# Last experts in steps of 1024 inner columns with 4 KB gate and up rows, 64 slots for the fifth place, one more ring place

## The chip, the core and the metric

The program runs on one core of a Trainium2 chip. The metric is the device time of one execution in microseconds (us). Before the change, three runs gave 2216.11, 2219.05 and 2222.17 us; their median is 2219.05 us. A change of under 0.3% (6.7 us) can't be told from none.

## What is computed

The reference passes 256 tokens of width 1024 (one x of 256 x 1024 in f32) through two blocks: a recurrent mixer and a first mixture of experts, then attention, a dense feed-forward layer, a state-space layer and a second mixture of experts. The change touches only this last layer:

```python
xt = _rms_norm(x, norm_g).reshape(-1, d)
logits = xt @ w_router                       # 256 tokens, 8 experts
top_vals, top_idx = lax.top_k(logits, 2)
gates = softmax(top_vals)
...
def expert_block(args):
    xb, e = args
    return (silu(xb @ w_gate[e]) * (xb @ w_up[e])) @ w_down[e]
...
out = segment_sum(ys * slot_w, slot_tok)
return x + out
```

w_gate and w_up are 1024 x 3584 per expert, w_down is 3584 x 1024, all f32: 44.04 MB for an expert, 352.3 MB for the eight. Each token goes to two of the eight experts, so the experts have 512 tokens in all.

## The kernel before

The last layer is the class `Moe2`. Tokens of one expert are gathered into slots (`gather`, a product with a 0/1 matrix), in blocks of 32: an expert has 2, 3 or 4 blocks, that is 64, 96 or 128 slots. The program is fixed ahead of the data, so the number of blocks belongs to a place in a ranking: expert 0 has place 0, the other seven have places 1 to 7 by falling number of tokens. `BLOCKS` gives the blocks by place, `PLACES` the order in which the places are worked through. In that order the experts have 3, 2, 4, 2, 3, 3, 2 and 3 blocks; they are called the first to the eighth here. Tokens that find no slot are counted (`n_over`), and if there are any, `general` computes them after the loop, with all experts' weights read again for each half of the tokens.

`experts` is the loop, 7 steps per expert, each over 512 of the 3584 inner columns. A step does these things in TensorE's order: half of the gate and up products (`project`, contraction over 512 of the 1024 features, two loads of 1 MB), the four transposes of the step before (`hidden_T`), the other half of gate and up, and then the down products of the step before (`down`, two loads). In between, ScalarE and VectorE make the hidden values of the step (`hidden`: silu of gate times up). A product has 32 slots as its stationary operand and 512 columns of weights as the moving one, and four of them run side by side in four column groups of the array. So the products of a step grow with the blocks: 144 matmul instructions for three blocks, 96 for two. For three blocks the third block's products take column groups of a second PSUM bank (L2710), and `third` copies half of that bank to SBUF, so that the two halves of its sums can be added.

All weights come through a ring of SBUF places of 8 KB per partition (1 MB in all), filled by SyncE's DMA queue in the order of the list that `loads` makes. A gate or up load takes 512 rows and 512 columns, so its contiguous runs in DRAM are 2 KB; a down load takes for each partition two adjacent rows of 1024 columns, 8 KB. A place is filled again as soon as its products are through (`done` calls `ahead`, which issues the next load); the ring has 15 places in this layer: 2 that are there from the start, 3 of the pool opened before the feed-forward layer, 4 of this layer's own (`K.slots(sp, 4, 3)` in `body`), and 6 that held split weights earlier.

PSUM has 8 banks: two hold an expert's output sums through all of its steps (one for two blocks), the gate and up sums take two (one) per 512 columns, and transposes, gathers and the combining products take one each. `combine` multiplies an expert's output by the gate weights and adds it to x, for the expert before during the second step of the next. After the last expert x is stored.

Of the kernel before, what the change touches and what calls it, by code (L numbers as in the profile page):

```python
# [2423 lines left out]
class Moe2(Phase):  # L2424
# [5 lines left out]
    BLOCKS = (3, 4, 3, 3, 3, 2, 2, 2)  # L2430
# [6 lines left out]
    def loads(cls, K):  # L2437
# [7 lines left out]
        def load(nm, e, k0, c0):  # L2445
            def fn(t):
                K.nc.sync.dma_start(t, expert(nm, e)[:, k0 * 128:(k0 + 4) * 128, c0:c0 + 512].rearrange("e (c p) f -> p (e c) f", p=128))  # L2447
                return 512
            return fn, False

        def rows(e, f, h):

            def fn(t):
                w = expert("down", e)[:, f * 512:(f + 1) * 512].rearrange("e (p q) c -> p (e q) c", q=4)
                K.nc.sync.dma_start(t.rearrange("p q c -> p (q c)").rearrange("p (q c) -> p q c", q=2), w[:, 2 * h:2 * h + 2])  # L2455
                return 512
            return fn, False

        steps = [(e, f) for e in range(cls.E) for f in range(7)]
        for s in range(len(steps) + 1):  # L2460
            if s < len(steps):
                e, f = steps[s]
                out += [load(nm, e, k0, f * 512) for k0 in (0, 4) for nm in ("gate", "up")]
            if s:
                out += [rows(*steps[s - 1], h) for h in range(2)]
# [9 lines left out]
    def route(self):  # L2475
# [9 lines left out]
        xT = K.rows_T(K.x, K.vec["moe_norm_2"], lambda: self.t("xT", [P, 8, P], 2))  # L2485
# [100 lines left out]
    def general(self):  # L2586
# [9 lines left out]
        with tc.If(self.n_over > 0):  # L2596
            for b in range(2):
                xw, hT = self.t("g_xn", [128, D], 2, tag="xg"), self.t("g_hT", [128, 8, 128], 2, tag="xT")
# [16 lines left out]
    def experts(self):  # L2615
        K = self.K
        n = 7 * self.E
# [4 lines left out]
        for s in range(n + 1):  # L2622
            e, f = s // 7, s % 7
            if s == 4:
                K.order += [K.nc.values_load(self.number[0:1, i:i + 1], engines=[mybir.EngineType.SP], min_val=0, max_val=self.E - 1) for i in range(1, self.E)]
            if s == 20:
                self.n_over = K.count(self.n_int)
            if f == 3 and e + 1 < self.E:
# [3 lines left out]
            if s < n:  # L2632
                gu = self.project(e)
                next(gu)
                next(nxt, None)
            if s:
                hid = self.hidden_T(hs.pop(s - 1), (s - 1) // 7)
            if s < n:
                hs[s] = self.hidden(drive(gu), e)
                next(nxt, None)  # L2640
            if s:
                self.down((s - 1) // 7, (s - 1) % 7, hid)
# [69 lines left out]
    def project(self, e):  # L2712
# [18 lines left out]
    def hidden(self, ps, e):  # L2731
        nc, nb = self.K.nc, self.blocks(e)
        h = self.t("h", [128, 512], 2)
        if nb == 4:
            nc.scalar.activation(h, ps[0], AF.Silu)
            nc.vector.tensor_tensor(h, h, ps[1], OP.mult)
            return h
        if nb == 3:
            t, g, u = self.third(ps[1]), self.t("third_g", [32, 512]), self.t("third_u", [32, 512])
            nc.vector.tensor_tensor(g, t[0:32], ps[1][0:32], OP.add)  # L2740
            nc.vector.tensor_tensor(u, t[32:64], ps[1][32:64], OP.add)
        nc.scalar.activation(h[0:64], ps[0][0:64], AF.Silu)  # L2742
        nc.vector.tensor_tensor(h[0:64], h[0:64], ps[0][64:128], OP.mult)  # L2743
        if nb == 3:
            nc.scalar.activation(g, g, AF.Silu)
            nc.vector.tensor_tensor(h[64:96], g, u, OP.mult)
        return h[0:32 * nb]

    def hidden_T(self, h, e):

        K, nc = self.K, self.K.nc
        S = 32 * self.blocks(e)
        p, hq = K.ps()[:, 0:4 * S], h.rearrange("s (p q) -> s q p", q=4)
        for j in range(4):
            nc.tensor.transpose(p[:, j * S:(j + 1) * S], hq[:, j], K.ident[0:S, 0:S])  # L2755
        hid = self.t("hid", [128, 4, 128], 2)[:, :, 0:S]
# [123 lines left out]
```

## Time and profile before

| | |
|---|---|
| runs | 2216.11, 2219.05, 2222.17 us |
| profiled execution, its own time | 2217.24 us |
| its span, first to last instruction | 2215.5 us |
| TensorE busy | 1965.2 us, 89% |
| VectorE, ScalarE, GpSimd busy | 730.1, 501.5, 165.1 us |
| DMA | 644.45 MB, mean 291 GB/s |
| granted clock, mean | 0.948 |

The profiled execution lies between the lowest run and the median, 1.8 us under the median. TensorE's busy time includes waits in the middle of a group, since ends of matmuls are modelled; the distance from one step's transposes to the next step's tells more than the busy share. The clock is a share of 2.4 GHz; 0.5 is the lower level, 1.2 GHz. The DMA share can read a little over 1, since packets of one engine overlap.

### The profile page before, as it was taken

Reading aid. Unit: us, or ns where it says so; the run is one execution under the profiler, and the core shown is the slowest. Engines: PE = TensorE matmul, PEld = TensorE weight load, DVE = VectorE, ACT = ScalarE, POOL = GpSimd, SP = SyncE. Lnnn points to the kernel's source line nnn. Section 1 sums busy time; section 2 is a strip of 40 time slices with the busy share of each in tenths; the row PEclk is TensorE's granted clock in tenths of the full one; section 3 lists DMA queues with packets and bytes.
Section 4 is the critical chain, followed back from the end, with each engine's and each line's share of the span. In section 5 each row is a group of like instructions: output and inputs, shape, how many; then the busy total and the mean of one; then the engine's idle time right before and its main releaser. Section 6 shows DMA issues by size and latency. Waiting matters only on the chain.

```text
span 2215.5 us, 35511 instructions
## 1 busy us (share of the span) xinstructions
PE 1965.2 (89%) x15104; PEld 1041.2 (47%) x15104; DVE 730.1 (33%) x1524; ACT 501.5 (23%) x917; POOL 165.1 (7%) x222
## 2 busy tenths in 40 slices
PE   7886888877777768889998689999999999999998
PEld 7765753323222356689997553333333333333232
DVE  6678841211201146554445732110001022211022
ACT  5452220100100035444444132110001111111111
POOL 3144100000000021000002410000000000000000
PEclk9998999989988989999999889999999999999999
DMA  6340459999999942165554099999989999999995
GB/s 201 116 136 20 154 190 362 421 419 390 419 418 420 408 141 96 58 219 186 179 188 153 1 337 358 387 397 397 392 286 398 397 396 398 396 398 397 398 394 222
DMA packets 220180, 644.45 MB, mean 291 GB/s; under 512 B 20606, under 2 KB 24108, under 8 KB 182124
## 3 DMA queue, kind: packets, MB, share of 16 engines
q1 hardware_dynamic: 219388, 641.13, 76.4%
q8 instruction: 122, 2.00, 0.4%
q0 software_dynamic: 336, 0.82, 0.1%
q14 instruction: 46, 0.38, 0.0%
q10 hardware_dynamic: 288, 0.13, 0.0%
HBM read 639.94 MB, written 1.05 MB: 289 GB/s over the span
## 4 chain that ended last, share of the span: by engine, by line
PE 51%; DVE 2%; DMA 1%; SPq 1%; POOL 0%; ACT 0%; issue 0%; POOLq 0%; ACTq 0%; DVEq 0%
PE ps L2705 28%; PE ps L2710 6%; PE ps L151 4%; PE ps L149 4%; PE ps L150 4%; PE ps L2755 1%; DMA w<-in_moe_w_up_dram 1%; PE ps L2789 1%; PE ps L2668 1%; DVE f L2356 1%; SPq L2447 1%; PE ps L2674 0%; DVE xs L2363 0%; SPq L2455 0%; PE ps L312 0%
## 5 line engine op out<-in xcount | busy, mean ns | idle before, releaser
L2705 PE MATMUL ps<-w,xg 128*32 128x512 f32 x4032 | 470.6, 594 | 4.7 <-DMA w<-in_moe_w_up_dram 3.7
L2705 PEld LDWEIGHTS ps<-w,xg 128*32 128x32 f32 x4032 | 124.4, 110 | 280.3 <-issue 260.5
L2705 PE MATMUL ps<-w,hid 128*32 128x512 f32 x2016 | 232.9, 593 | 0.6 <-ACT hid L2757 0.6
L120 DVE TENSOR_TENSOR wl<-w,wh 128x1024 fp32r<-128x1024 f32 (+1 forms) x146 | 174.2, 1237 | 179.7 <-ACT wh L119 179.7
L1547 PE MATMUL ps<-w,xg 128*32 128x512 f32 x1024 | 163.8, 674 | 51.3 <-DMA w<-in_moe_w_up_dram 42.0
L149 PE MATMUL ps<-hT,wh 128*128 128x256 f32 x704 | 204.8, 291 | 2.9 <-ACT wh L119 1.9
L151 PE MATMUL ps<-hT,wl 128*128 128x256 f32 x704 | 203.4, 289 | 0.5 <-DVE wl L120 0.5
L150 PE MATMUL ps<-hT,wh 128*128 128x256 f32 x704 | 203.2, 289 | 0.0
L119 ACT ACTIVATE wh<-w 128x1024 fp32r<-128x1024 f32 (+1 forms) x148 | 146.8, 1044 | 199.7 <-PE ps L150 110.1
L149 PEld LDWEIGHTS ps<-hT,wh 128*128 128x128 f32 x704 | 139.4, 198 | 4.5 <-ACT wh L119 2.3
L150 PEld LDWEIGHTS ps<-hT,wh 128*128 128x128 f32 x704 | 139.3, 198 | 0.3
L151 PEld LDWEIGHTS ps<-hT,wl 128*128 128x128 f32 x704 | 138.8, 197 | 0.8 <-DVE wl L120 0.8
L2740 DVE TENSOR_TENSOR third_g<-third,ps 32x512 f32<-32x512 f32 x28 | 18.9, 676 | 356.2 <-ACT third L2728 356.2
L2705 PEld LDWEIGHTS ps<-w,hid 128*32 128x32 f32 x2016 | 64.3, 110 | 145.5 <-issue 139.1
L1547 PE MATMUL ps<-w,hidT 128*32 128x512 f32 x512 | 96.0, 724 | 41.0 <-DMA w<-in_moe_w_down_dram 35.1
L2710 PE MATMUL ps<-w,xg 128*32 128x512 f32 x896 | 119.9, 592 | 0.0
L1547 PEld LDWEIGHTS ps<-w,xg 128*32 128x32 f32 x1024 | 36.8, 121 | 161.1 <-issue 73.8
L2743 DVE TENSOR_TENSOR h<-h,ps 64x512 f32<-64x512 f32 x49 | 33.8, 690 | 224.0 <-ACT h L2742 223.2
L2757 ACT ACTIVATE hid<-ps 128x384 f32<-128x384 f32 (+2 forms) x56 | 26.0, 463 | 354.5 <-PE ps L2755 354.2
L1547 PEld LDWEIGHTS ps<-w,hidT 128*32 128x32 f32 x512 | 20.8, 126 | 105.2 <-DMA w<-in_moe_w_down_dram 58.6
L1514 PEld LDWEIGHTS ps<-oh,xn 128*128 128x128 f32 x256 | 62.2, 334 | 16.2 <-issue 13.7
L1514 PE MATMUL ps<-oh,xn 128*128 128x128 f32 x256 | 65.3, 412 | 4.4 <-PEq L1457 3.5
(667 smaller groups left out, 2358.6 us busy)
## 6 DMA issues: line engine op xcount, KB each, us to landing
w<-in_moe_w_gate_dram SPq DMA_DIRECT2D x176, 1024.0 KB
w<-in_moe_w_up_dram SPq DMA_DIRECT2D x176, 1024.0 KB
w<-in_moe_w_down_dram SPq DMA_DIRECT2D x176, 1024.0 KB
w<-in_dffn_w_gate_dram SPq DMA_DIRECT2D x14, 1024.0 KB
w<-in_dffn_w_up_dram SPq DMA_DIRECT2D x14, 1024.0 KB
w<-in_dffn_w_down_dram SPq DMA_DIRECT2D x14, 1024.0 KB
w<-in_w_in_dram SPq DMA_DIRECT2D x12, 1024.0 KB
w<-in_att_w_in_dram SPq DMA_DIRECT2D x6, 1024.0 KB
```

The costliest lines, as they stand in the source:

```text
L119: self.nc.scalar.activation(hi, src, AF.Copy)
L120: (engine or self.nc.vector).tensor_tensor(lo, src, hi.bitcast(F32), OP.subtract)
L149: mm(out, lhs[0], rhs[0], start=first, stop=False)
L150: mm(out, lhs[0], rhs[1], start=False, stop=False)
L151: mm(out, lhs[1], rhs[0], start=False, stop=last)
L1514: nc.tensor.matmul(p[:, k4], xn[b][:, 4 * kk + k4], oh[:, b].rearrange("p e s -> p (e s)"), start=(b == 0), stop=(b == 1))
L1547: nc.tensor.matmul(p[j * C:(j + 1) * C, :], lhs[:, k, j * C:(j + 1) * C], part(ws[j], i, c), start=(k == 0), stop=(k == n - 1))
L2356: nc.vector.tensor_tensor_scan(fl(f[:, r, c, pairs]), fl(self.rhos[:, pairs]), fl(f[:, r, c, pairs]), 0.0, op0=OP.mult, op1=OP.add)
L2705: mm(o, lhs[:, k + i, 32 * c:32 * c + 32], rhs[i][m], start=(begin and k + i == 0), stop=(end and k + i == n - 1))
L2710: mm(ps[1][r:r + 32], lhs[:, k + i, 64:96], rhs[i][m], start=(begin and k == 0), stop=(end and k == n - 2))
L2743: nc.vector.tensor_tensor(h[0:64], h[0:64], ps[0][64:128], OP.mult)
L2757: nc.scalar.activation(hid, p.rearrange("p (j s) -> p j s", j=4), AF.Copy)
```

## The change

- `BLOCKS` gives the fifth place (index 4), which is worked through last, 2 blocks where it had 3. The blocks in order are now 3, 2, 4, 2, 3, 3, 2, 2.
- `STEPS = (2, 2, 2, 1)`: an expert has four steps, three over 1024 inner columns and one over 512. Gate and up loads of the former take 256 rows and 1024 columns, in runs of 4 KB; a load is still 1 MB. The two banks of gate and up sums of a three-block expert become four in such a step.
- A step's down rows are 8 next to each other per partition (32 KB) where they were 4 (16 KB); each load still takes two of them, 8 KB. A down place is given back after each load, no longer after two.
- `hidden` runs over the two halves of a step one after the other, and adds the third block's gate sums in place, in the buffer that `third` copied to. `hidden_T` makes eight transposes, two groups of four for three and four blocks, one group of eight for two.
- The ring has a sixteenth place (`K.slots(sp, 5, 3)`). The route's `xT` shares the buffers of `hid`.
- The gather of the next expert starts at its third step (of four), with one more point per step at which a piece of it can run; the order of the experts is read at step 2 (it was 4), the overflow count at step 12 (20).

```diff
-    BLOCKS = (3, 4, 3, 3, 3, 2, 2, 2)
+    BLOCKS = (3, 4, 3, 3, 2, 2, 2, 2)
+    STEPS = (2, 2, 2, 1)
...
-        def load(nm, e, k0, c0):
+        def load(nm, e, k0, c0, n):
             def fn(t):
-                K.nc.sync.dma_start(t, expert(nm, e)[:, k0 * 128:(k0 + 4) * 128, c0:c0 + 512].rearrange("e (c p) f -> p (e c) f", p=128))
+                w = expert(nm, e)[:, k0 * 128:(k0 + 4 // n) * 128, c0 * 512:(c0 + n) * 512].rearrange("e (c p) f -> p (e c) f", p=128)
+                K.nc.sync.dma_start(t.rearrange("p q c -> p (q c)").rearrange("p (q c) -> p q c", c=n * 512), w)
...
-        def rows(e, f, h):
+        def rows(e, c0, n, h):
-                w = expert("down", e)[:, f * 512:(f + 1) * 512].rearrange("e (p q) c -> p (e q) c", q=4)
+                w = expert("down", e)[:, c0 * 512:(c0 + n) * 512].rearrange("e (p q) c -> p (e q) c", q=4 * n)
...
     def experts(self):
-        n = 7 * self.E
+        K, F = self.K, len(self.STEPS)
+        n = F * self.E
...
-            if f == 3 and e + 1 < self.E:
+            if f == 2 and e + 1 < self.E:
...
             if s < n:
-                hs[s] = self.hidden(drive(gu), e)
+                ps = drive(gu)
+                next(nxt, None)
+                hs[s] = self.hidden(ps, e)
...
-        ps = [K.ps() for _ in range(1 if nb == 2 else 2)]
-        for k0 in (0, 4):
-            ws = K.take(2)
-            for k in (0, 2):
-                self.products(nb, ps, self.cur[e]["xg"], k0 + k, [[w[:, k + i, :] for w in ws] for i in range(2)], 8)
+        ps = [[K.ps() for _ in range(1 if nb == 2 else 2)] for _ in range(n)]
+        r = 4 // n
+        for k0 in range(0, 8, r):
+            ws = [w.rearrange("p q c -> p (q c)").rearrange("p (q c) -> p q c", q=r) for w in K.take(2)]
+            for c in range(n):
+                for k in range(0, r, 2):
+                    self.products(nb, ps[c], self.cur[e]["xg"], k0 + k, [[w[:, k + i, c * 512:(c + 1) * 512] for w in ws] for i in range(2)], 8)
...
-    def hidden(self, ps, e):
+    def hidden(self, banks, e):
+        whole = self.t("h", [128, 1024], 2)
+        for c, ps in enumerate(banks):
+            h = whole[:, c * 512:(c + 1) * 512]
...
+                t, u = self.third(ps[1]), self.t("third_u", [32, 512])
+                g = t[0:32]
+                nc.vector.tensor_tensor(u, t[32:64], ps[1][32:64], OP.add)
+                nc.vector.tensor_tensor(g, g, ps[1][0:32], OP.add)
...
     def down(self, e, f, hid):
-        ws = K.take(2)
-        for h, w in enumerate(ws):
-            self.products(nb, s["py"], hid, 2 * h, [[w[:, 2 * i + m, :] for m in range(2)] for i in range(2)], 4, f == 0, f == 6)
-        K.done(2)
+        q = hid.shape[1]
+        for k in range(0, q, 2):
+            w = K.take()[0]
+            self.products(nb, s["py"], hid, k, [[w[:, 2 * i + m, :] for m in range(2)] for i in range(2)], q, f == 0, last)
+            K.done()
...
-            K.slots(sp, 4, 3)
+            K.slots(sp, 5, 3)
```

SyncE's queue holds the loads. Before, one step of the first expert, behind its first steps (w are ring places):

```order
L2447 DMA w_9931<-in_moe_w_gate_dram 128x4x512
L2447 DMA w_9971<-in_moe_w_up_dram 128x4x512
L2447 DMA w_9973<-in_moe_w_gate_dram 128x4x512
L2447 DMA w_10014<-in_moe_w_up_dram 128x4x512
L2455 DMA w_10016<-in_moe_w_down_dram 128x2048
L2455 DMA w_10052<-in_moe_w_down_dram 128x2048
```

Of the change, the end of the second step and the last step of that expert:

```order
L2451 DMA w_9885<-in_moe_w_gate_dram 128x2x1024
L2451 DMA w_9887<-in_moe_w_up_dram 128x2x1024
L2459 DMA w_9913<-in_moe_w_down_dram 128x2048
L2459 DMA w_9915<-in_moe_w_down_dram 128x2048
L2459 DMA w_9941<-in_moe_w_down_dram 128x2048
L2459 DMA w_9943<-in_moe_w_down_dram 128x2048
L2451 DMA w_9992<-in_moe_w_gate_dram 128x4x512
L2451 DMA w_10006<-in_moe_w_up_dram 128x4x512
L2451 DMA w_10020<-in_moe_w_gate_dram 128x4x512
L2451 DMA w_10034<-in_moe_w_up_dram 128x4x512
```

Four down loads stand together where two did, and gate and up have the shape 2 x 1024 but for the last step, which is as before.

TensorE, in the eighth expert: before, the end of a pair of gate and up loads, the transposes of the step before and the begin of the next pair (ps are PSUM banks, xg the gathered tokens, h the hidden values):

```order
L2710 MATMUL ps_15185<-w_14937,xg_14390 32x512
L2710 MATMUL ps_15185<-w_14974,xg_14390 32x512
L2755 MATMUL ps_15210<-ident,h_15147 128x96 x4
L2705 MATMUL ps_15184<-w_14976,xg_14390 32x512 x2
L2705 MATMUL ps_15184<-w_15004,xg_14390 32x512 x2
L2705 MATMUL ps_15184<-w_14976,xg_14390 32x512 x2
L2705 MATMUL ps_15184<-w_15004,xg_14390 32x512 x2
L2710 MATMUL ps_15185<-w_14976,xg_14390 32x512
L2710 MATMUL ps_15185<-w_15004,xg_14390 32x512
L2710 MATMUL ps_15185<-w_14976,xg_14390 32x512
```

The change in the same place:

```order
L2711 MATMUL ps_14972<-w_14812,xg_14404 32x512 x2
L2711 MATMUL ps_14972<-w_14802,xg_14404 32x512 x2
L2711 MATMUL ps_14972<-w_14812,xg_14404 32x512 x2
L2770 MATMUL ps_14990<-ident,h_14935 128x64 x8
L2711 MATMUL ps_14972<-w_14822,xg_14404 32x512 x2
L2711 MATMUL ps_14972<-w_14832,xg_14404 32x512 x2
L2711 MATMUL ps_14972<-w_14822,xg_14404 32x512 x2
L2711 MATMUL ps_14972<-w_14832,xg_14404 32x512 x2
```

The rows of L2710, the third block, are gone there, and the transposes have 64 columns where they had 96 and are eight in one group.

The third place follows at once in TensorE's order, the end of gate and up and the down products of the step before (hid are the transposed hidden values). Before:

```order
L2705 MATMUL ps_15184<-w_15004,xg_14390 32x512 x2
L2710 MATMUL ps_15185<-w_14976,xg_14390 32x512
L2710 MATMUL ps_15185<-w_15004,xg_14390 32x512
L2710 MATMUL ps_15185<-w_14976,xg_14390 32x512
L2710 MATMUL ps_15185<-w_15004,xg_14390 32x512
L2705 MATMUL ps_14832<-w_15006,hid_15215 32x512 x8
L2710 MATMUL ps_14833<-w_15006,hid_15215 32x512 x4
L2705 MATMUL ps_14832<-w_15039,hid_15215 32x512 x8
L2710 MATMUL ps_14833<-w_15039,hid_15215 32x512 x4
```

Of the change:

```order
L2711 MATMUL ps_14972<-w_14822,xg_14404 32x512 x2
L2711 MATMUL ps_14972<-w_14832,xg_14404 32x512 x2
L2711 MATMUL ps_14972<-w_14822,xg_14404 32x512 x2
L2711 MATMUL ps_14972<-w_14832,xg_14404 32x512 x2
L2711 MATMUL ps_14793<-w_14864,hid_14989 32x512 x8
L2711 MATMUL ps_14793<-w_14866,hid_14989 32x512 x8
L2711 MATMUL ps_14793<-w_14895,hid_14989 32x512 x8
L2711 MATMUL ps_14793<-w_14897,hid_14989 32x512 x8
```

A pair of loads ends without the third block, and four down loads with 8 products each stand where two with 12 stood.

## Rows read from the trace of the kernel before

**Rows 1.** The page's 40 slices of the span, each about 55.4 us.

```profile
PE   7886888877777768889998689999999999999998
...
DMA  6340459999999942165554099999989999999995
```

**Rows 2.** Table by stretch, one row per expert; stretch, length, busy us, PEclk, DMA share, GB/s.

```profile
1322.70:1435.90 113.20, 113.20 (x1016) 36.30 (x1012) 22.59 (x50) 20.45 (x37) 0.18 (x1) 1.00 1.00 374
1435.90:1531.60 95.70, 95.70 (x826) 31.53 (x822) 8.36 (x15) 10.15 (x20) 0.00 (x0) 1.00 1.03 397
1531.60:1676.80 145.20, 145.20 (x1307) 45.80 (x1303) 8.11 (x15) 11.88 (x21) 0.00 (x0) 1.00 0.95 353
1676.80:1767.00 90.20, 90.20 (x778) 29.58 (x774) 10.33 (x18) 11.07 (x22) 0.00 (x0) 1.00 1.04 397
1767.00:1886.30 119.30, 119.30 (x1067) 38.22 (x1063) 23.93 (x38) 20.20 (x36) 0.00 (x0) 1.00 1.03 396
1886.30:2002.10 115.80, 115.80 (x1019) 37.16 (x1015) 22.06 (x35) 18.77 (x34) 0.00 (x0) 1.00 1.04 397
2002.10:2101.60 99.50, 94.81 (x779) 30.18 (x775) 10.34 (x18) 11.07 (x22) 0.00 (x0) 1.00 1.03 398
2101.60:2195.90 94.30, 94.30 (x850) 29.85 (x848) 18.94 (x28) 13.82 (x24) 0.00 (x0) 1.00 0.94 363
```

**Rows 3.** The same table: first MoE layer; third expert; fourth to seventh expert.

```profile
400.00:500.00 100.00, 78.19 (x389) 30.97 (x388) 23.63 (x61) 10.84 (x17) 0.00 (x0) 0.88 1.01 419
1600.00:1675.00 75.00, 75.00 (x690) 24.03 (x690) 3.15 (x6) 7.11 (x13) 0.00 (x0) 1.00 0.87 312
1680.00:2050.00 370.00, 370.00 (x3218) 119.86 (x3214) 62.56 (x103) 55.60 (x103) 0.00 (x0) 1.00 1.04 397
```

**Rows 4.** Timeline, TensorE, two steps apart each; start us, duration us.

```profile
1691.60 0.69 PE L2755 MATMUL ps<-ident,h 64*128 64x64 f32 x4
1702.66 0.69 PE L2755 MATMUL ps<-ident,h 64*128 64x64 f32 x4
...
2152.37 0.72 PE L2755 MATMUL ps<-ident,h 96*128 96x96 f32 x4
2168.61 0.72 PE L2755 MATMUL ps<-ident,h 96*128 96x96 f32 x4
```

**Rows 5.** Waits between 2002 and 2102 us; total us, times, longest.

```profile
PE ps L2705 <- DMA w<-in_moe_w_up_dram: 3.7, 4, 1.7
```

**Rows 6.** Timeline, last products to the store of the result.

```profile
2195.94 0.72 PE L2755 MATMUL ps<-ident,h 96*128 96x96 f32 x4
2201.56 1.04 PE L2710 MATMUL ps<-w,hid 128*32 128x512 f32 x8
2202.72 0.59 ACT L2728 ACTIVATE third<-ps 64x512 f32<-64x512 f32 x1 [5.53 <-PE ps L2710]
2203.33 1.21 ACT L2781 ACTIVATE y<-ps 64x512 f32<-64x512 f32 x2
2203.34 1.39 DVE L2782 TENSOR_TENSOR y<-third,ps 32x512 f32<-32x512 f32 x2 [8.91 <-ACT third L2728]
2204.17 5.36 PE L2789 MATMUL ps<-y,cwT 96*128 96x512 f32 x8 [1.57 <-DVE y L2782]
2210.33 0.41 SPq L2859 DMA_DIRECT2D out_dram<-x  x1
```

**Rows 7.** Timeline, ScalarE and VectorE between two steps of the last expert.

```profile
2158.50 0.59 ACT L2728 ACTIVATE third<-ps 64x512 f32<-64x512 f32 x1 [4.88 <-PE ps L2710]
2159.12 0.68 DVE L2740 TENSOR_TENSOR third_g<-third,ps 32x512 f32<-32x512 f32 x1 [13.42 <-ACT third L2728]
2159.83 0.68 DVE L2741 TENSOR_TENSOR third_u<-third,ps 32x512 f32<-32x512 f32 x1
2159.84 0.63 ACT L2745 ACTIVATE third_g<-third_g 32x512 f32<-32x512 f32 x1
2161.27 0.68 DVE L2746 TENSOR_TENSOR h<-third_g,third_u 32x512 f32<-32x512 f32 x1
```

More of the change, by code (lines that the diff above doesn't have):

```diff
@@ L2457, in rows @@
             return fn, False
-        steps = [(e, f) for e in range(cls.E) for f in range(7)]
+        steps = [(e, sum(cls.STEPS[:f]), n) for e in range(cls.E) for f, n in enumerate(cls.STEPS)]
         for s in range(len(steps) + 1):
             if s < len(steps):
-                e, f = steps[s]
-                out += [load(nm, e, k0, f * 512) for k0 in (0, 4) for nm in ("gate", "up")]
+                e, c0, n = steps[s]
+                out += [load(nm, e, k0, c0, n) for k0 in range(0, 8, 4 // n) for nm in ("gate", "up")]
             if s:
-                out += [rows(*steps[s - 1], h) for h in range(2)]
+                out += [rows(*steps[s - 1], h) for h in range(2 * steps[s - 1][2])]
         return out
@@ L2729, in third @@
         return t
-    def hidden(self, ps, e):
+    def hidden(self, banks, e):
         nc, nb = self.K.nc, self.blocks(e)
[L2733 to L2747, printed above, removed]
+        whole = self.t("h", [128, 1024], 2)
+        for c, ps in enumerate(banks):
+            h = whole[:, c * 512:(c + 1) * 512]
+            if nb == 4:
+                nc.scalar.activation(h, ps[0], AF.Silu)
+                nc.vector.tensor_tensor(h, h, ps[1], OP.mult)
+                continue
+            if nb == 3:
+                t, u = self.third(ps[1]), self.t("third_u", [32, 512])
+                g = t[0:32]
+                nc.vector.tensor_tensor(u, t[32:64], ps[1][32:64], OP.add)
+                nc.vector.tensor_tensor(g, g, ps[1][0:32], OP.add)
+            nc.scalar.activation(h[0:64], ps[0][0:64], AF.Silu)
+            nc.vector.tensor_tensor(h[0:64], h[0:64], ps[0][64:128], OP.mult)
+            if nb == 3:
+                nc.scalar.activation(g, g, AF.Silu)
+                nc.vector.tensor_tensor(h[64:96], g, u, OP.mult)
+        return whole[0:32 * nb, 0:512 * len(banks)]
@@ L2749, in hidden_T @@
     def hidden_T(self, h, e):
         K, nc = self.K, self.K.nc
[L2752 to L2756, printed above, removed]
-        nc.scalar.activation(hid, p.rearrange("p (j s) -> p j s", j=4), AF.Copy)
+        S, q = 32 * self.blocks(e), h.shape[1] // 128
+        hq = h.rearrange("s (p q) -> s q p", q=q)
@@ L2758, in hidden_T @@
+        hid = self.t("hid", [128, 8, 128], 2)[:, 0:q, 0:S]
+        n = 4 if S > 64 else q
+        for j0 in range(0, q, n):
+            p = K.ps()[:, 0:n * S].rearrange("p (j s) -> p j s", j=n)
+            for j in range(n):
+                nc.tensor.transpose(p[:, j], hq[:, j0 + j], K.ident[0:S, 0:S])
+            nc.scalar.activation(hid[:, j0:j0 + n], p, AF.Copy)
         return hid
@@ L2762, in down @@
         K, nc, s, nb = self.K, self.K.nc, self.cur[e], self.blocks(e)
+        last = f == len(self.STEPS) - 1
         if f == 0:
             s["py"] = [K.ps() for _ in range(1 if nb == 2 else 2)]
[L2765 to L2769 removed]
+        q = hid.shape[1]
[3 more added lines that the diff above has]
+            K.done()
+        if not last:
             return
```

20 lines of the change are left out of this document (9 added, 11 removed).

## The prediction

> **What bounds the kernel now.** I read the slices of the page first [rows 1]: from the 24th slice on both TensorE and the DMA engines show 9 in nearly every slice. That is the last layer, some 900 us, and only there does the change act. Two engines at 9 cannot both be the limit at every moment, so I cut the stretch at the first transposes of each expert [rows 2]. The transposes stand 7 per expert in the timeline, so each row runs from an expert's first step to the next one's.
>
> The spans follow the blocks, not the bytes: 113 to 119 us for three blocks, 145.2 for four, 90.2 for two, though each expert moves the same 44.04 MB. So TensorE sets the pace, with the granted clock at 1.00, the 2.4 GHz level, throughout. At the same time DMA runs at 396 to 398 GB/s and a share of 1.03 or 1.04 in most rows, so it is full too; it falls under 0.9 only inside the third expert [rows 3], where the ring has no free place. The ring carries credit: what is loaded ahead under four blocks is eaten under two. It runs out once: the seventh expert takes 99.5 us where the fourth, of the same shape, takes 90.2, and TensorE waits for loads there [rows 2, 5]. So both bounds are within a few per cent of each other, and a change of one needs the other.
>
> **TensorE's side.** Two steps with three blocks are 16.24 us apart, with two blocks 11.06 [rows 4]. The eighth expert goes from three to two: 7 x 5.18 = 36.3 us less. The other experts keep their products. The price of one product is (16.24 - 11.06) / 48 = 0.108 us. A step of 144 has 0.7 us beside its products, as long as its four transposes (0.72 us [rows 4]); they are not fewer in longer steps, so merging steps saves TensorE next to nothing.
>
> **DMA's side.** At 397 GB/s six loads (four gate and up, two down; 6.29 MB) take 15.85 us, and an expert's 42 take 110.9. The first MoE layer loads in runs of 8 KB alone and gets 419 GB/s [rows 3], 2.503 us for 1 MB. Down loads have 8 KB runs too, so the 2 KB loads get the rest: (15.85 - 5.01) / 4 = 2.711 us. Per run and engine that is 84.7 ns for 2 KB and 312.9 ns for 8 KB. No row shows a 4 KB run. It lies between these ends, 2.503 and 2.711 us for 1 MB; a straight line through both (8.7 ns per run and 76.1 ns per 2 KB) gives 160.8 ns, **2.573 us a load**, which I take. Then an expert's loads take 24 x 2.573 + 4 x 2.711 + 14 x 2.503 = 107.6 us.
>
> **The sum.** Credit is counted in us of loads ahead of TensorE. Before, from the end of the third expert: the fourth eats 110.9 - 90.2 = 20.7, the fifth earns 119.3 - 110.9 = 8.4, the sixth 4.9, the seventh eats 20.7, together -28.1; the trace shows 9.3 us short, so a full ring was worth 18.8 us (7 of 15 loads, the rest being in use or in flight). One more place adds a load: 21.4. With the change: 21.4 - 17.4 = 4.0 after the fourth; + 11.7 = 15.7; + 8.2, capped at 21.4; - 17.4 = 4.0 after the seventh. So the 9.3 us of waits go, and the eighth expert's first transposes come at 2101.6 - 9.3 = 2092.3 us.
>
> There 304 of 336 loads are taken by the new order. The 32 left take 14 x 2.573 + 4 x 2.711 + 14 x 2.503 = 81.9 us, less the credit 77.9: the last lands at 2170.2. TensorE's own work would be through by about 2164 (six steps of 11.06 and the last down products), so here **loads become the bound** and some 6 us of the 36.3 stay unused. Behind the last load come 16 products, 1.7 us, so 2171.9. The end of the last products before is 2202.6, and the span's end 12.9 us later [rows 6]; two blocks need one copy of the output in place of three copies and two additions, 0.9 us less: 12.0. The span ends at 2183.9, 31.6 us earlier than 2215.5. The profiled execution's own time is 2217.24, so it would be 2185.6; it lies 1.8 us under the median of the runs shown, and against that median I predict **2187.5 us**.
>
> With 4 KB at 2.711 us the same sum gives no credit for the seventh expert (6.6 us of waits), a last load at 2182.7 and 19.1 us less: 2200. With 2.503 it gives 34.1 us less: 2185.
>
> **What else moves.** Seven reads of the experts' order stand on SyncE's queue at nearly the same load as before, in the first expert, where the DMA share is 1.00 [rows 2]; the loads queued ahead hide them, and without that cover they would cost a few us that a three-block expert's TensorE time takes up. `hidden` now does two halves in turn. One half takes from 2158.50 to 2161.95, 3.45 us [rows 7], and since g lies in the buffer of `third` the second half cannot start earlier: 6.9 us. TensorE meanwhile does the down products of the step before (96 products, 10.4 us, for three blocks; 5.2 behind a step of 512) and the next step's first pair (48 products, 5.2), so 10.3 us of cover at the least; only the layer's very first step has 5.2, a loss of 1.7 us once, at a time when the ring is full anyway. Banks: four for the sums, two for the output, two left for transposes; the next step's second two wait for `hidden` at worst 1.7 us behind a short step, and the 2.6 us of the pair's first half cover that.
>
> **Rivals.**
>
> (A) 4 KB rows bring little: the cost of a run is not a fixed part plus bytes. Half the way to no gain gives 2194, all of it 2200. For it: the same engines show a share over 1 with 2 KB runs, so part of a run's fixed cost already overlaps the next. Against: 397 against 419 GB/s, both at a full share [rows 3]. The Trainium skill (DMA: Bandwidth & Descriptors, "Why small descriptors are slow") names a fixed overhead of about three cycles per packet beside 32 bytes a cycle, 67 cycles for 2 KB and 131 for 4 KB; by that a load would take 2.650 us and the sum would give 2194, an estimate from that page. The trace has a larger step between 2 and 8 KB (8%) than that rule (3.5%).
>
> (B) TensorE's clock falls when it waits for loads in the eighth expert. In the first MoE layer, where loads bound, TensorE is busy 78 of 100 us and the mean granted clock is 0.88 [rows 3]; in the seventh expert it is busy 94.8 of 99.5 us and keeps 1.00 [rows 2]. The 71 us left of the eighth expert take 81 us at 0.88, 2 us past the loads. **Slower than before** it becomes only if the mean clock there is under 0.64: 71 / 0.64 = 111 us, as much as the 2092.3 to 2203.5 us that make no change. The rows stand against it, for the waits are short ones of about 1 us. The Trainium skill (TensorE: Matmul & The Clock Gate, "HAM oscillation") warns of just this, matmuls that wait for DMA and start again at half clock; the first MoE layer agrees, the seventh expert does not.
>
> (C) `hidden` or the banks hold TensorE up at every step of three and four blocks. The 16 steps of the four such experts would need 2 us each to eat the whole gain; against it stand the 10.3 us of cover.
>
> (D) The fifth place holds more than 64 tokens. Then `general` runs and reads all weights twice, 705 MB, at 397 GB/s 1775 us more. With the seed that the reference draws by itself, its router gives expert 0 53 tokens and the others 108, 84, 71, 57, 54, 54 and 31: the fifth place has 57. It decides at 65.
>
> **Chances.** The forecast, with 4 KB runs near the line and loads as the late bound: 0.66. (A): 0.16. (B): 0.06, a third of it slower. (C): 0.08, of which 0.03 within 0.3% and 0.01 slower. (D): 0.02. 4 KB runs as good as 8 KB ones or better: 0.02. That makes faster by over 0.3% 0.92, within 0.3% (6.7 us, what a measurement can't tell from none) 0.03, slower 0.05. The range takes in the forecast, (A) up to its end at 2200 and the bound at 2185, with 3 us on either side, the distance of the runs shown from their median: 2182 to 2203.
>
> **What would show it.** Each of the first seven experts' spans as before within 2 us, the seventh near 90 without waits; the eighth near 80 us with TensorE waiting for loads; DMA at about 408 GB/s over the fourth to the seventh; a share under 1 in the third expert and now also at the end of the sixth; `third_u` never ending a wait of TensorE. It is wrong if DMA stays at 397, if the eighth expert's clock falls under 0.9, or if the first three experts grow longer.

## The result, and the profile after

The kernel before took 2218.57 us (median of 4 runs, 2216.11 to 2222.17), the changed one **2185.04 us** (4 runs, 2181.78 to 2189.87). The ratio is 0.9849, 95% interval 0.9826 to 0.9872: 33.5 us less. The forecast was 2187.5 us with a range of 2182 to 2203. The profiled execution of the change took 2184.64 us, its span is 2182.9 us.

The slices of the page, to be laid beside [rows 1] (below them the GB/s that DMA moved):

```profile
PE   7886889767777768789998779999999999999986
...
DMA  6330449999999963065555159999989999999997
GB/s 204 117 124 34 150 180 349 398 419 387 420 417 420 415 214 123 1 222 191 177 192 174 39 226 377 362 412 408 411 308 359 408 411 408 411 405 404 409 412 308
```

Both engines show 9 from the 25th slice on, but for an 8 of DMA in the 30th. What is new is at the end: the last slices of TensorE are 8 and 6 now, and DMA stands at 9 up to the last but one. The GB/s show where loads were not made: 308 and 359 in the third expert.

The table by expert, to be laid beside [rows 2] and [rows 3]; same columns, the last row is the fourth to the seventh expert. The first transposes stand later in an expert than before (behind a step of 1024 columns, not 512), so a row answers to its own of before only where the experts on both sides have as many blocks; the sums over all rows can be compared.

```profile
1333.90:1443.30 109.40, 108.60 (x985) 35.42 (x981) 20.69 (x48) 19.65 (x36) 0.17 (x1) 1.00 0.99 379
1443.30:1544.60 101.30, 101.30 (x891) 33.56 (x887) 8.28 (x15) 9.24 (x17) 0.00 (x0) 1.00 1.02 410
1544.60:1681.70 137.10, 137.10 (x1242) 43.63 (x1239) 8.02 (x15) 11.22 (x21) 0.00 (x0) 1.00 0.92 349
1681.70:1774.20 92.50, 92.50 (x811) 30.66 (x807) 12.29 (x21) 11.35 (x21) 0.00 (x0) 1.00 1.02 409
1774.20:1892.40 118.20, 118.20 (x1064) 38.19 (x1063) 23.84 (x38) 20.06 (x36) 0.00 (x0) 1.00 1.02 411
1892.40:2003.60 111.20, 111.20 (x982) 36.02 (x982) 19.93 (x32) 17.45 (x32) 0.00 (x0) 1.00 1.01 404
2003.60:2090.80 87.20, 85.21 (x731) 28.49 (x727) 8.22 (x15) 8.80 (x17) 0.00 (x0) 1.00 1.02 409
2090.80:2166.90 76.10, 63.85 (x513) 20.41 (x513) 6.02 (x9) 4.75 (x8) 0.00 (x0) 1.00 1.01 406
1680.00:2050.00 370.00, 370.00 (x3262) 120.86 (x3250) 62.21 (x103) 53.27 (x97) 0.00 (x0) 1.00 1.02 408
```

DMA moves 408 GB/s where it moved 397. The third expert still has a share of 0.92, and in the sixth the rate dips from 411 to 404. In the eighth TensorE is busy 63.85 of 76.1 us, and the granted clock is 1.00 nevertheless. What TensorE waited for there, to be laid beside [rows 5]:

```profile
PE ps L2711 <- DMA w<-in_moe_w_up_dram: 7.4, 6, 1.6
PE ps L2711 <- DMA w<-in_moe_w_down_dram: 2.0, 4, 0.6
PE ps L2711 <- SPq L2600: 2.0, 2, 1.4
PE ps L2711 <- DMA w<-in_moe_w_gate_dram: 0.9, 1, 0.9
```

12.3 us, all of it for loads. (The third row has no load's name, because SyncE has issued the last loads by then and stands at the branch of line 2600. The two waits are those of down products at 2162.49 and 2164.99 below; the trace has landings at 2162.44 and 2164.94, so they are loads too.) Two pairs of gate and up products in that expert show the pace of the loads themselves (timeline, TensorE):

```profile
2097.41 3.64 PE L2711 MATMUL ps<-w,xg 128*32 128x512 f32 x32 [1.17 <-DMA w<-in_moe_w_up_dram]
2102.51 3.20 PE L2711 MATMUL ps<-w,xg 128*32 128x512 f32 x26 [1.46 <-DMA w<-in_moe_w_up_dram]
```

Each began when the second of its two loads of 4 KB runs had landed, 5.10 us apart: 2.55 us a load. The end of the kernel, to be laid beside [rows 6]:

```profile
2162.49 1.92 PE L2711 MATMUL ps<-w,hid 128*32 128x512 f32 x16 [1.38 <-SPq L2600]
...
2164.99 1.92 PE L2711 MATMUL ps<-w,hid 128*32 128x512 f32 x16 [0.58 <-SPq L2600]
...
2166.84 0.69 PE L2770 MATMUL ps<-ident,h 64*128 64x64 f32 x4
...
2168.07 3.79 PE L2711 MATMUL ps<-w,hid 128*32 128x512 f32 x32 [0.54 <-ACT hid L2771]
...
2169.93 0.16 PEld L2711 LDWEIGHTS ps<-w,hid 128*32 128x32 f32 x8 [0.84 <-SPq L2600]
...
2172.57 1.99 PE L2805 MATMUL ps<-y,cwT 64*128 64x512 f32 x8 [0.72 <-ACTq L2600]
```

The second half of the last 32 products could only begin at 2169.93, when the last load was there (landed at 2169.88). They end at 2171.86, and 11.0 us later the span ends.

### The profile page after: what moved, and what is told of

Read it like the earlier page. It is cut to its first block, busy times and chain, and to the rows that moved or that the text cites. A ratio compares the mean times of both kernels' runs of the same rounds, so it can differ in the third digit from the quotient of the medians.

```text
span 2182.9 us, 34847 instructions
## 1 busy us (share of the span) xinstructions
PE 1911.5 (88%) x14768; PEld 1029.8 (47%) x14768; DVE 713.4 (33%) x1501; ACT 486.2 (22%) x889; POOL 165.0 (8%) x222
## 5 line engine op out<-in xcount | busy, mean ns | idle before, releaser
L2711 PE MATMUL ps<-w,xg 128*32 128x512 f32 x4032 | 463.3, 594 | 10.3 <-DMA w<-in_moe_w_up_dram 8.8
L2711 PEld LDWEIGHTS ps<-w,xg 128*32 128x32 f32 x4032 | 127.9, 110 | 296.8 <-issue 265.3
L1547 PE MATMUL ps<-w,xg 128*32 128x512 f32 x1024 | 163.2, 665 | 58.2 <-DMA w<-in_moe_w_up_dram 47.3
L1547 PE MATMUL ps<-w,hidT 128*32 128x512 f32 x512 | 89.0, 654 | 42.0 <-DMA w<-in_moe_w_down_dram 36.0
L1547 PEld LDWEIGHTS ps<-w,xg 128*32 128x32 f32 x1024 | 37.7, 118 | 165.8 <-DMA w<-in_moe_w_up_dram 75.4
L2751 DVE TENSOR_TENSOR third_u<-third,ps 32x512 f32<-32x512 f32 x21 | 14.3, 679 | 238.7 <-ACT third L2736 238.7
L2716 PE MATMUL ps<-w,xg 128*32 128x512 f32 x672 | 87.5, 592 | 0.0
L2771 ACT ACTIVATE hid<-ps 128x384 f32<-128x384 f32 (+2 forms) x44 | 22.5, 527 | 270.3 <-PE ps L2770 270.3
```

Source lines behind the costliest of these rows:

```text
L1547: nc.tensor.matmul(p[j * C:(j + 1) * C, :], lhs[:, k, j * C:(j + 1) * C], part(ws[j], i, c), start=(k == 0), stop=(k == n - 1))
L2711: mm(o, lhs[:, k + i, 32 * c:32 * c + 32], rhs[i][m], start=(begin and k + i == 0), stop=(end and k + i == n - 1))
L2716: mm(ps[1][r:r + 32], lhs[:, k + i, 64:96], rhs[i][m], start=(begin and k == 0), stop=(end and k == n - 2))
L2771: nc.scalar.activation(hid[:, j0:j0 + n], p, AF.Copy)
```

## The experiments

All times are medians; the ratio to the kernel before, measured on the same chip beside each, is the safer number.

**The parts of the change, one at a time.** First the change without the smaller eighth expert.

```
-    BLOCKS = (3, 4, 3, 3, 2, 2, 2, 2)
+    BLOCKS = (3, 4, 3, 3, 3, 2, 2, 2)
```

> The change with the fifth place back at 96 slots (three blocks), all else as changed. Theory (two bounds: the longer rows and the 16th place give the loads credit, which is worth only what TensorE waited for): no expert waits for loads, the seventh place in the order takes about 90 us, and the eighth is bound by TensorE, so the gain over the kernel before is its 9.3 us of waits and little else: 2207 to 2211 us, about 24 us over the change. The last weight load lands over 10 us before the last products. Rival 1 (the loads alone set the end, the block fewer is worth nothing): as the change, 2185. Rival 2 (the block fewer is all of it, rows and place bring nothing): as before, 2218, with the seventh expert's waits still there.

Measured: 2198.45 us, ratio 0.9914 (0.9900 to 0.9927), 19 us less than before and not some 9, so the theory's number is missed. No wait for loads is left (its eighth expert shows a DMA share of 0.88), so neither rival holds; but TensorE gained about 9 us that the theory has no place for. The run f1 below finds them.

The kernel before with the 64 slots alone:

```
-    BLOCKS = (3, 4, 3, 3, 3, 2, 2, 2)
+    BLOCKS = (3, 4, 3, 3, 2, 2, 2, 2)
```

> The kernel before with 64 slots for the fifth place and nothing else: 2 KB rows, steps of 512, 15 places. Theory: the seventh expert runs out of loads as before (99 to 100 us), and the eighth, two blocks now, is bound by its loads, which went on landing until 2189.8 us in the kernel before and can come only about 2 us sooner: products end near 2192, and the time is 2205 to 2209 us, a third of the 36.3 us that TensorE is relieved of. Rival 1 (TensorE alone sets the end): 36 us less than before, 2182. Rival 2 (loads alone): within 3 us of before, 2216 to 2219.

Measured: 2207.03 us, ratio 0.9954 (0.9940 to 0.9967), as the theory has it. Its seventh and eighth expert (table by stretch, columns as above):

```profile
2003.90:2101.60 97.70, 91.10 (x731) 28.36 (x727) 8.30 (x15) 9.63 (x20) 0.00 (x0) 0.98 1.03 397
2101.60:2190.80 89.20, 78.75 (x579) 24.63 (x577) 6.71 (x10) 5.84 (x12) 0.00 (x0) 0.96 1.01 390
```

The seventh runs short as before, and the eighth, a third lighter for TensorE, is 5 us shorter only, with 10.4 us idle. Of the 36.3 us of the block, 10 reach the end.

The change with 2 KB runs. The places hold other columns, and the products of a step follow in the order of its loads:

```
-                w = expert(nm, e)[:, k0 * 128:(k0 + 4 // n) * 128, c0 * 512:(c0 + n) * 512].rearrange(...)
+                kk, c = k0 // 4 * 4, c0 + k0 % 4 // 2
+                K.nc.sync.dma_start(t, expert(nm, e)[:, kk * 128:(kk + 4) * 128, c * 512:(c + 1) * 512].rearrange(...))
...
```

> The change with gate and up loaded in runs of 2 KB again (4 x 512 columns in a place), steps, slots and places as changed, and the same products in another order within a step. Theory: a load of such rows takes 2.711 us in place of 2.573, the five experts behind the third get 24 x 0.138 = 3.3 us less credit each, the seventh expert waits 5 to 8 us, the last load lands near 2182: 2197 to 2201 us, DMA at 397 GB/s. Rival 1 (the run's length does nothing, the longer steps or the eight down rows do): as the change, 2185. Rival 2 (TensorE's two blocks are all of it): as the change, 2185, with DMA at 397 GB/s.

Measured: 2200.18 us, ratio 0.9923 (0.9909 to 0.9936), as the theory has it. Fourth to seventh expert, then the seventh:

```profile
1680.00:2050.00 370.00, 369.14 (x3234) 119.67 (x3226) 62.21 (x103) 53.70 (x98) 0.00 (x0) 1.00 1.03 397
2000.60:2103.20 102.60, 92.35 (x731) 29.09 (x727) 8.23 (x15) 8.80 (x17) 0.00 (x0) 0.98 1.03 396
```

The rate falls back to 397 GB/s with the run's length (the reordered products move the same bytes), and the seventh expert takes 102.6 us where it took 87.2, 10.3 of them idle where 5 to 8 were expected. The 4 KB rows are worth 15 us beside the smaller expert. Beside 96 slots no run has them alone; f1 below, with faster loads still, shows that only 10 us of waits are there to be saved.

The change with the ring of before:

```
-            K.slots(sp, 5, 3)
+            K.slots(sp, 4, 3)
```

> The change with 15 ring places, as before. Theory: one load less of credit from the first expert on, 2.6 us: 2186 to 2189 us, of it a few us of new waits in the seventh expert, the eighth bound by loads as with 16. Rival 1 (the place is what lets the loads run through the seventh expert): 2192 or more. Rival 2 (the place does nothing, because the ring is full only where nobody waits): 2185, within a microsecond.

Measured: 2185.54 us, ratio 0.9856 (0.9841 to 0.9871). The time can't be told from that of the change; it lies under the theory's range and on rival 2's number. The trace speaks for the theory: from the seventh expert's first transposes to the last ones this kernel takes 166.0 us (2004.4 to 2170.4), the change 163.3 (2003.6 to 2166.9) and, in its second run g1 below, 163.0 (2003.3 to 2166.3).

**Where the 9 us come from.** The kernel before, gate and up read in 8 KB runs (other weights; the runs of a load then lie end to end):

```
-                K.nc.sync.dma_start(t, expert(nm, e)[:, k0 * 128:(k0 + 4) * 128, c0:c0 + 512].rearrange(...))
+                j = c0 // 256 + k0 // 4
+                w = expert(nm, e).rearrange("e k f -> e (k f)")[:, j * 262144:(j + 1) * 262144].rearrange("e (p c) -> p (e c)", p=128)
+                K.nc.sync.dma_start(t.rearrange("p q c -> p (q c)"), w)
```

> The kernel before with gate and up loads that read the same number of bytes in runs of 8 KB: the weights they read are other ones, so the outputs are not the reference's; steps of 512, 15 places, 96 slots for the fifth place stay. The question is what the kernel with 96 slots (2198.5 us) gained beyond the 9.3 us of waits. Theory 1 (longer steps save TensorE itself some 7.5 us, in joints between transposes, gathers and products): here, with the old steps and no wait for loads, only the waits go: 2206 to 2210 us, experts one to six as long as before, the seventh 90 to 91. Theory 2 (small waits for loads all along, which the view doesn't name, were what went): 2197 to 2201, the first six experts shorter by about 1 us each.

Measured: 2207.44 us, ratio 0.9955 (0.9940 to 0.9970): theory 1. The first to the seventh expert, and the seventh, of this kernel, then of the one with longer steps and 96 slots (e1); the eighth expert's first step has three blocks in both, so the stretches are alike:

```profile
1323.10:2092.70 769.60, 769.60 (x6764) 248.18 (x6760) 105.72 (x189) 103.62 (x192) 0.18 (x1) 1.00 0.97 391
...
2002.50:2092.70 90.20, 90.20 (x778) 29.61 (x774) 10.34 (x18) 11.06 (x22) 0.00 (x0) 1.00 1.01 420
```

```profile
1334.40:2096.60 762.20, 761.40 (x6765) 248.05 (x6761) 105.36 (x190) 100.33 (x184) 0.18 (x1) 1.00 1.00 394
```

TensorE is busy throughout in both, but for 0.8 us, and 7.4 us are gone over seven experts: 1.06 us an expert. The first six experts of f1 take 679.4 us (1323.1 to 2002.5), as long as before (1322.7 to 2002.1 [rows 2]) though loads are faster, so no small waits for loads went there, and theory 2 falls. One sees in the timelines at which joints, that is changes between products and transposes or gathers, TensorE saves. Before, then the change:

```profile
1702.66 0.69 PE L2755 MATMUL ps<-ident,h 64*128 64x64 f32 x4
1703.28 3.64 PE L2705 MATMUL ps<-w,xg 128*32 128x512 f32 x32
...
1707.22 1.09 PE L2770 MATMUL ps<-ident,h 64*128 64x64 f32 x8
1708.25 10.51 PE L2711 MATMUL ps<-w,xg 128*32 128x512 f32 x96
```

Eight transposes hold the products up for 1.03 us (1707.22 to 1708.25); before, four held them up for 0.62 us (1702.66 to 1703.28), with 96 slots for 0.65. There are three such pairs in an expert, some 0.25 us each. The gather of the fourth expert's time is one group of eight products now, 2.03 us from its begin to the next products (1718.68 to 1720.71), and was two of four, 1.09 and 1.10 us (from 1706.85 and from 1711.51). Together that is 0.9 of the 1.06 us, an estimate from these rows.

**One place more, and another order.** The change with 17 places (one buffer for h and one for y make the room; two smaller edits, not shown, give other tiles that shared these buffers a place):

```
-            K.slots(sp, 5, 3)
+            K.slots(sp, 6, 3)
...
-        whole = self.t("h", [128, 1024], 2)
+        whole = self.t("h", [128, 1024])
...
-        y, p = self.t("y", [128, 2, 512], 2), s["py"]
+        y, p = self.t("y", [128, 2, 512]), s["py"]
```

> The change with 17 ring places (one buffer each for the hidden values and for the experts' outputs makes the room). Theory: one load more of credit from the first expert on, 2.6 us less at the last load: 2181 to 2184 us, TensorE waiting some 2.6 us less in the eighth expert, which is still bound by loads. Rival 1 (a place is worth nothing, as the medians of the kernel with 15 say): 2185 within a microsecond. Rival 2 (one buffer for the hidden values holds TensorE up at each step): 2187 or more, with waits for ScalarE ahead of the transposes or the products.

Measured: 2181.69 us, ratio 0.9835 (0.9820 to 0.9851). From the seventh expert's first transposes to the last ones it takes 161.8 us (2003.0 to 2164.8), 1.5 less than the change. They lie in the seventh expert (85.5 us and not 87.2) and not, as expected, in the eighth (76.3 and 76.1). No wait for ScalarE has come in but one of 0.5 us, which the change has as well.

The change with another order of the places:

```
-    PLACES = (0, 5, 1, 6, 2, 3, 7, 4)
+    PLACES = (0, 5, 2, 6, 1, 7, 3, 4)
```

> The change with another order of the places: blocks 3, 2, 3, 2, 4, 2, 3, 2 where they are 3, 2, 4, 2, 3, 3, 2, 2. Theory: the time is set by loads that were not made while the ring was full (DMA share 0.92 in the third expert, over 10 us, and some at the end of the sixth); two and three blocks in turn leave the ring emptier when the four blocks come, so fewer are lost, and the last load lands 5 to 12 us sooner: 2173 to 2180 us, with a few us of waits in the fourth expert and fewer in the eighth. Rival 1 (four blocks overfill the ring wherever they stand, so as much is lost): 2185, within 2 us. Rival 2 (the waits of the fourth expert come on top): 2188 or more.

Measured: 2179.55 us, ratio 0.9825 (0.9811 to 0.9839), as the theory has it. The fourth, fifth and eighth expert:

```profile
1646.30:1756.40 110.10, 104.49 (x890) 34.38 (x886) 8.28 (x15) 9.24 (x17) 0.00 (x0) 1.00 1.02 410
1756.40:1893.60 137.20, 137.20 (x1243) 43.73 (x1239) 8.02 (x15) 11.21 (x21) 0.00 (x0) 1.00 0.95 364
...
2095.60:2162.00 66.40, 61.96 (x517) 20.86 (x513) 6.21 (x9) 4.74 (x8) 0.00 (x0) 1.00 1.01 404
```

The expert with four blocks stands fifth here. It finds the ring empty (TensorE waits 5.6 us just ahead of it) and lets more be loaded, 364 GB/s and not 349; the dip of the sixth is gone as well. Fewer loads are left for the end, where 4.4 us of idle stand for 12.3.

Both together:

> The last two together: the new order of places and 17 ring places. Theory: their gains add, as both are loads made sooner, until TensorE is the bound; without any wait TensorE's products would end near 2158 us of the change's profile (2171.9 less 14.3 us of waits), 14 us before it: 2170 to 2177 us. Rival 1 (TensorE is the bound already with the new order): as that order alone, within a microsecond. Rival 2 (neither does anything): 2185.

Measured: **2173.63 us**, ratio 0.9808 (0.9792 to 0.9823), the fastest of those that load the reference's weights: 43 us under the kernel before, and under the change 9 by the ratios and 11 by the medians. So the gains add, as the theory has it: beside the new order the seventeenth place is worth 6 us by the medians, though the two intervals overlap, and the trace shows 2.4 us less in the fourth expert and 2.5 in the eighth (its rows stand with g3 below).

**How much faster loads can give.** The change itself again, and then two kernels with gate and up in 8 KB runs (other weights; the edit is as in f1, in the change's load function):

> The change itself, once more, beside the two below. All theories: 2185 us. It settles what a ring place is worth: with 15 places 2185.5 and with 17 places 2181.7 us were measured; at 2.6 us a place the change has to lie between them, near 2184.

Measured: 2185.34 us, ratio 0.9846 (0.9832 to 0.9859). With 15, 16 and 17 places the ratios are 0.9856, 0.9846 (0.9849 the first time) and 0.9835: about 2.3 us a place, near the 2.6 of theory, though the three intervals overlap. The traces show it more surely: 166.0, 163.0 to 163.3 and 161.8 us from the seventh expert's first transposes to the last ones.

> The change with gate and up loads that read the same number of bytes in runs of 8 KB (other weights, so the outputs are not the reference's). Theory (the ring is full again at the end of the sixth expert, so what faster loads earn before it is capped there): only the loads of the last two experts count, 48 x 0.07 us: 3 to 4 us less, 2180 to 2183 us, with TensorE still waiting for loads in the eighth expert and a lower DMA share in the sixth. Rival 1 (every load behind the third expert counts): five experts, 8.4 us less: 2176 to 2178. Rival 2 (the loads are no bound any more): 2185.

Measured: 2177.94 us, ratio 0.9817 (0.9797 to 0.9838): 6 to 7 us less, more than the 3 to 4 expected, and on rival 1's number. The trace decides otherwise. Its fifth, sixth and seventh expert:

```profile
1772.80:1891.00 118.20, 118.20 (x1067) 38.22 (x1063) 23.83 (x38) 20.04 (x36) 0.00 (x0) 1.00 1.01 419
1891.00:2002.20 111.20, 111.20 (x986) 36.08 (x982) 19.93 (x32) 17.43 (x32) 0.00 (x0) 1.00 0.98 391
2002.20:2085.80 83.60, 83.60 (x731) 27.78 (x727) 8.22 (x15) 8.79 (x17) 0.00 (x0) 1.00 1.01 420
```

In the sixth the rate falls to 391 GB/s, from 419 in the fifth; the change has 404 there, from 411. What the faster loads earned is lost there to the full ring, as the theory has it. The theory's size was too small. My arithmetic had left out the four loads of each expert that have 2 KB runs in the change (0.21 us each by the price of the prediction): 24 x 0.07 + 4 x 0.21 = 2.5 us for an expert, 5.0 for the last two. The trace shows 5.5: first transposes of the seventh expert to the last transposes are 157.8 us (2002.2 to 2160.0) where the change has 163.3 (2003.6 to 2166.9). By the same arithmetic rival 1 would give 12.5. (This is worked out after the run. With 2.55 us for a 4 KB load, as measured, the two come to 3.9 and 9.8 us; the trace stays nearer to the theory.)

> The new order of places and 17 ring places, with gate and up loads in runs of 8 KB as in the last one (other weights). Theory: the 7 us in which TensorE still waited for loads there (5.2 for gate and up, 2.1 for down) go and nothing more, since TensorE is then the bound from the first expert to the last: 2166 to 2169 us. Rival 1 (loads still bound, all that they save counts): 2160 to 2165. Rival 2 (its waits are no longer on the path): 2173.6 as with 4 KB.

Measured: 2161.01 us, ratio 0.9735 (0.9721 to 0.9749): 12.6 us less than with 4 KB by the medians (the ratios, from two chips, make it 16; the profiles' spans 12.4), not 7, and on rival 1's number. TensorE's waits in this kernel from the third expert to the last transposes, all of them, and its fourth and eighth expert, then the same two with 4 KB (kernel f4):

```profile
PE ps L2806 <- ACTq L2601: 0.7, 1, 0.7
PE ps L2712 <- ACT hid L2772: 0.5, 1, 0.5
```

```profile
1644.10:1745.40 101.30, 101.30 (x891) 33.59 (x887) 8.29 (x15) 9.24 (x17) 0.00 (x0) 1.00 1.01 420
...
2084.60:2143.40 58.80, 58.80 (x513) 19.40 (x513) 6.20 (x9) 4.74 (x8) 0.00 (x0) 1.00 0.99 409
```

```profile
1644.60:1752.30 107.70, 103.70 (x891) 34.78 (x887) 8.29 (x15) 9.24 (x17) 0.00 (x0) 1.00 1.02 410
...
2091.40:2155.30 63.90, 61.15 (x517) 20.56 (x513) 6.20 (x9) 4.75 (x8) 0.00 (x0) 1.00 1.00 403
```

No wait for a load is left, so TensorE is the bound here, as the theory has it and rival 1 does not. But with 4 KB the fourth and eighth expert took 6.4 and 5.1 us more, 11.5 in all, while the waits by name were 6.9 us up to the last products: the theory's 7 us were waits by name. The rest was in rows that count as busy. Two rows of the change's eighth expert show how:

```profile
2116.32 1.05 PE L2711 MATMUL ps<-w,xg 128*32 128x512 f32 x4
2117.66 3.63 PE L2711 MATMUL ps<-w,xg 128*32 128x512 f32 x28 [0.29 <-DMA w<-in_moe_w_up_dram]
```

Four products at 0.108 us each take 0.43 us, so the next could have begun at 2116.75; it began at 2117.66, 0.9 us later, and 0.29 us of that is called a wait. The row ahead of a wait is shown with the whole length of its last product (594 ns on the page), which the next product otherwise overlaps. In f4 that makes 4.7 us for eight waits, 0.6 us each. What loads cost TensorE is read from the length of a stretch against the same stretch without waits.

**The runs together.** From the ratios, times 2218 us, each line with one thing more than the line above (e1 and f1 differ in ring places and in the length of the runs as well, which I take to make no difference where TensorE waits for no load; for the runs the first six experts of f1 show it):

| step | kernel | us against before | step's worth |
|---|---|---|---|
| waits for loads gone | f1 | -10 | 10 |
| longer steps | e1 | -19 | 9 |
| eighth expert with two blocks, still no waits | g3 | -59 | 40 |
| the loads as they are in the change | the change | -34 | 25 given back |

g3 has another order of places too; without waits the order only permutes TensorE's work. TensorE could have ended 59 us sooner, and the loads let 34 of it through. By the medians of g1 and g3, which ran side by side, the last step is 24 us, and by the traces 22.3: first to last transposes take 810.7 us in g3 (1332.7 to 2143.4) and 833.0 in the change.

## Why the prediction was right

**The bound at the end: right.** It said that the loads become the bound in the eighth expert, and that is what the waits, the share of 1.01 and the runs e3, f2, f3 and g2 show: what brings loads sooner brings the end sooner (f2 by its trace, since its time alone can't be told from the change), and what slows them (e3) brings it later.

**The price of a 4 KB load: right.** 2.573 us by a straight line between 2 and 8 KB; 2.55 measured in the eighth expert, and 411 GB/s in the fifth where 2 KB gave 396. From 411: (107.2 - 4 x 2.711 - 14 x 2.503) / 24 = 2.55 us. Rival (A) falls. The rule of the Trainium skill that stood beside it (DMA: Bandwidth & Descriptors, "Why small descriptors are slow") gave 2.650 us, an estimate. The trace has a smaller figure: from 2 to 4 KB a load gets 6% cheaper (2.711 to 2.55 us) and by the rule 2%, so more of a load's time goes by the number of runs than the rule's three cycles. What that is worth here, e3 shows.

**The ring place: right in size.** 2.6 us said; 2.3 by the ratios, whose intervals overlap, and between 1.2 and 3.0 by the traces.

**`hidden` on two halves: right.** In the fifth expert the two halves run from 1826.77 to 1833.67, 6.9 us as worked out:

```profile
1826.77 0.59 ACT L2736 ACTIVATE third<-ps 64x512 f32<-64x512 f32 x1
1827.39 0.59 ACT L2753 ACTIVATE h<-ps 64x512 f32<-64x512 f32 x1
...
1830.24 0.59 ACT L2736 ACTIVATE third<-ps 64x512 f32<-64x512 f32 x1 [0.75 <-DVE h L2757]
...
1832.99 0.68 DVE L2757 TENSOR_TENSOR h<-third,third_u 32x512 f32<-32x512 f32 x1
```

The 0.75 us in the third row is the second half held up by the first, on ScalarE; TensorE meanwhile has 10.4 us of down products (1826.98 to 1837.41), and no wait of TensorE's on `third_u` appears. Rival (C) falls, with it (D): `general` did not run.

**"Merging steps saves TensorE next to nothing": wrong.** It saves 1.06 us an expert, 8.5 in all (f1 against e1). I had priced the transposes by their number, which longer steps leave as it is, and not by how long a group of them holds the products up: 1.03 us for eight, and 2 x 0.62 for two times four.

**"Some 6 us of the 36.3 stay unused": wrong.** 22 us do. Two terms on TensorE's side were left out: the 8.5 us above, and 5.2 us of the eighth expert's third block that lie ahead of its first transposes (three pairs of loads with 16 products less each, 48 x 0.108), which I left in 2092.3. 6 + 8.5 + 5.2 is 19.7 of the 22.3 measured; where the other 2.6 are stays open. The forecast time hardly shows it, because loads were the bound in the eighth expert anyway; what came through of the longer steps is the next point.

**The last load, 2170.2 against 2169.93: right by luck.** I took 2092.3 as the time of the eighth expert's first transposes by the old steps and the 304 loads taken there by the new ones, which stand two pairs of loads later. Counted alike, from the seventh expert: its first transposes by the new steps come 2 x 32 x 0.108 = 6.9 us behind 2002.1, at 2009.0; 74 loads are left there, 81.9 + 107.6 = 189.5 us, less the 21.4 of a full ring: 2177.1. The time would have been forecast at 2194.4, still in the range and 9 us too high. What made up for it is mostly the longer steps, the term I had put at nothing: the seventh expert's first transposes came at 2003.6, 5.4 us before 2009.0. TensorE's pace does count up to there, since it sets when the ring is full; from there on only loads count. The rest is the price of a load (2.555 us makes 188.8 of the 189.5) and the credit (188.8 less the 166.3 us up to the last load: 22.5, not 21.4). Behind the last product 11.0 us followed where 12.0 were said, and the median of the runs lies 0.4 us over the profiled execution where 1.8 were added; these two make the 2.5 us between 2187.5 and 2185.04.

**Rival (B), the clock: fell.** In the eighth expert of the change, with waits of 1.6 us at most, the granted clock is 1.00, all at the 2.4 GHz level; it was 0.98 when the change ran again (g1), and 0.96 in e2, with 10.4 us idle. In the first MoE layer it is 0.93 in the change where [rows 3] has 0.88, with the same work. Some hundredths, then, and where loads are the bound they cost nothing: from the seventh expert's first transposes to the last ones g1 takes 163.0 us and the first profile 163.3. The fall to half clock of which the Trainium skill warns (TensorE: Matmul & The Clock Gate, "HAM oscillation") is not seen in the eighth expert of the first profile, and is seen in g1's, where the granted clock is 0.50 between 2149 and 2151 us. No wait of TensorE's by name is longer than 1.6 us there either, so the prediction's argument that the waits are short ones did not hold for every execution; what held is that the loads hide the loss.

**The signs.** DMA moved 408 GB/s over the fourth to the seventh expert, as said, and the eighth took 76.1 us (near 80 said), waiting for loads. The first seven experts kept their sum less the steps' saving; the seventh was "near 90 without waits" only in part (87.2 with 2.0 us idle, 83.6 without waits in g2); the dip at the end of the sixth is there in GB/s (404 against 411) and not in the share. In [rows 1] TensorE shows 9 from the 25th slice on, and not from the 24th; nothing hangs on it.

## What to carry to other kernels

Where two bounds lie within a few per cent, the worth of an edit is not its own saving: 64 slots alone gave 10 us, the loads' side alone (with the longer steps) 19, both 34, and without any wait for loads 59 would have come. Ask for each bound at which place a buffer is full, since what is earned before it is lost there, and move the long piece of work to where the buffer is empty (here one table of numbers, 5 us). And count a sum that runs over an edit in the same units on both sides of it: I mixed positions of the old and the new steps and was saved by a second error.

## What the runs showed of the hardware that I had not expected

- With gate and up loads in runs of 2, 4 and 8 KB an expert's loads move 397, 410 and 420 GB/s, at shares of 1.03, 1.02 and 1.01. The price of 1 MB is 2.71, 2.55 and 2.50 us: a little under a straight line of time per run against length at 4 KB.
- A change from products to transposes and back costs TensorE a part that does not grow with their number: four transposes hold the products up for 0.62 us, eight for 1.03, so by these two some 0.2 us a time, an estimate. Over an expert such joints were worth 1.06 us.
- TensorE's busy time contains waits: in f4 6.9 us of waits had a name, and 11.5 us were there, some 0.6 us more for each wait.
- The same kernel, with no wait by name over 1.6 us either time, kept a granted clock of 1.00 through its last expert in one execution and fell to 0.50 for a stretch of it in another (g1); from the seventh expert's first transposes to the last ones it took 163.3 and 163.0 us.
